# A hybrid trunk with RWKV-7 heads on one core: two pairs of heads per step, eight matrices per inverse

## The chip, the cores and the metric

One core of one Trainium2 chip runs the whole program. The metric is the device time of one execution in microseconds (us), lower is better. The engines are named as in the profile: PE (TensorE, matrix products), PEld (its weight loads), DVE (VectorE), ACT (ScalarE), POOL (GpSimd) and SP (SyncE, which issues the DMAs). PE writes into PSUM banks of 512 fp32 numbers per partition, and the other engines read them from there.

## The reference

A decoder trunk of two layers, width 2048, 256 tokens, all in float32. Each layer is a sequence mixer and a feed-forward part, each followed by a residual addition and a layer normalisation. Layer 0 mixes with multi-head latent attention (8 heads) and RWKV-7 (16 heads of 64), layer 1 with a gated DeltaNet and retention. The change is about the RWKV-7 heads, which the reference computes one token at a time:

```python
def step(st, inp):
    r_t, w_t, k_t, v_t, a_t, b_t = inp
    sa = jnp.einsum('bhvk,bhk->bhv', st, a_t)
    st = st * w_t[:, :, None, :] + sa[..., None] * b_t[:, :, None, :] + v_t[..., None] * k_t[:, :, None, :]
    return st, jnp.einsum('bhvk,bhk->bhv', st, r_t)
```

`r`, `k` and `v` are projections of the input, mixed with the token before (a shift); the decay `w`, the rate inside `b` and a gate `g` come from three low-rank projections. The result of each head is normalised over its 64 numbers (group norm), gets a bonus term from r, k and v, is multiplied with the gate and goes through the output projection together with the attention heads.

## The kernel before

Weights. All weights stream from HBM in blocks of eight 128x128 tiles into three buffers (`wr`), issued by SP. ACT rounds each half block to `wh` (L264), DVE or POOL computes the rest `wl` (L268), and PE makes three matmuls with 256 columns for each tile (L358 to L360): the stream. A group of 16 tiles of depth ends in one of two PSUM banks with the tag `mm`.

RWKV heads. `pair_mix` treats a pair of heads (128 partitions) at a time, over the 256 tokens in two chunks of 128. Its stages, each ended by a `yield`:

- `lw`, `la`, `lg` (L1094 to L1101): low-rank products for decay, rate and gate; ACT takes tanh; DVE sums the decay along time (two scans); ACT's exponentials give `e1`, `e2`. From these come `rAR`, `rb0`, `rkt` and `rt3`.
- Score products `rbig` (L1147): for each head, which takes one half of the 128 rows (partitions 0 to 63 or 64 to 127), a tile of one bank with both chunks. ACT copies and scales, POOL masks them into `rNB` and `rKA`.
- `tri_inv`: the inverse of the four 128x128 unit triangular matrices (2 heads x 2 chunks). ACT and POOL gather the 32x32 diagonal blocks, four small DMAs (L735) lay them out on 16 partitions, DVE eliminates in 14 steps of two instructions (L753, L754), four DMAs (L760) bring them back, and six `step`s of small matmuls (`tps`, L774) with DVE work between them assemble the inverse `tri_xt`: four with 32x32 blocks, two with 64x64.
- `rG`, `ru`, `rS`, `ry` (L1180 to L1207): chunk by chunk the products with the inverse, the state `rST` between the chunks, the output `ry`.
- Group norm on DVE (L1254 to L1261), transposes `ryt` (L1213), the bonus `rbon` (L1217), the gate and the split into `o0h` and `o0l`, which are inputs of the output projection.

The banks of PSUM: `c0` and `c1` with two each, one tag for even and one for odd pairs, `sm` two, `mm` two. `run_rolling` keeps two pairs alive at once, started 11 steps apart; each runs at a high priority, and one step of the attention heads (`side`) is taken in between. The program is put in order by a tile scheduler that takes the instructions of the highest priority that are ready by its model, so that stream matmuls stand between the stages of the pairs. Most buffers of `pair_mix` are double, r, k and v triple (`shift`, tag `sh_r` and so on).

Output projection. `out_part` multiplies some of the 16 input tiles with the weights and adds the result to `xf` on DVE (L854). The parts: tiles 0 to 3 and 4 to 7 (attention) within the attention heads, 8 to 11 behind the fourth pair, 12 and 13 behind the last, and last 14 and 15, in which the sums of the layer normalisation are taken along for each of the 16 columns (on POOL `accE`, L422; the column's split for the next phase, `rawl`, L537).

Mixer 1 uses `tri_inv` too, with four matrices at a time.

Of the kernel before, what the change touches and what calls it, by code (L numbers as in the profile page):

```python
# [16 lines left out]
P = 128  # L17
# [256 lines left out]
class K:  # L274
# [55 lines left out]
    def bank(self, tag, name):  # L330
        return self.psum.tile([P, 512], F32, name=name, tag=tag, bufs=self.banks[tag])
# [15 lines left out]
    LAG0 = 11  # L347
    LAG1 = 9
    BANKS0 = dict(c1=2, c0=2, sm=2, mm=2)
# [356 lines left out]
    def tri_persist(self, pool, n):  # L706
        v = self.nc.vector
        self.tri_slots = []
        for i in range(n):
            xt = pool.tile([P, 4, P], F32, name=f"tri_xt{i}")  # L710
            v.memset(xt, 0.0)
            x64 = pool.tile([64, 4, 64], F32, name=f"tri_x64{i}")
            v.memset(x64, 0.0)
            self.tri_slots.append((xt, x64))
        self.tri_n = 0

    def tri_inv(self, pool, nt, name, bank):


# [7 lines left out]
        c32 = pool.tile([P, 4, 32], F32, name=f"tc_{name}", tag="tc", bufs=1)  # L727
# [5 lines left out]
        q = pool.tile([16, self.QW], F32, name=f"tq_{name}", tag="tq", bufs=1)  # L733
        for h in range(4):
# [10 lines left out]
        for s in range(1, 15):  # L745
            n = 15 - s
            tmp = pool.tile([16, 2, 8, 8], F32, name=f"te_{name}_{s}", tag="te", bufs=2)
            t4 = tmp.rearrange("p k a b -> p k (a b)")[:, :, :s * n].rearrange("p k (c t) -> p k c t", c=s)
            z = qk[:, :, 0:512].rearrange("p k (c t) -> p k c t", t=32)
            col = z[:, :, 0:s, s:s + 1].broadcast_to([16, 2, s, n])  # L750
            row = qk[:, :, 32 * s + s + 1:32 * s + 16].unsqueeze(2).broadcast_to([16, 2, s, n])
# [6 lines left out]
        zc = pool.tile([P, 4, 32], F32, name=f"tz_{name}", tag="tc", bufs=1)  # L758
        for h in range(4):
            nc.sync.dma_start(zc[:, h, :], q[4 * h:4 * h + 4, :1024].rearrange("b (s t) -> b s t", t=32))  # L760
        x = pool.tile([P, 4, 32], F32, name=f"tx_{name}", tag="tx", bufs=2)
# [7 lines left out]
        def step(nm, n, ops):  # L769
            ps = bank(f"tps_{name}_{nm}")  # L770
            o = ps[:, :4 * n].rearrange("p (h c) -> p h c", h=4)
            for po, lhs, rhs in ops:
                for h in range(4):
# [4 lines left out]
        vv = pool.tile([P, 4, 32], F32, name=f"tv_{name}_16", tag="tv", bufs=2)  # L778
        v.tensor_tensor(vv, o, self.c("lev16x").unsqueeze(1).broadcast_to([P, 4, 32]), ALU.mult)
# [7 lines left out]
        vv = pool.tile([P, 4, 32], F32, name=f"tv_{name}_32", tag="tv", bufs=2)  # L787
# [4 lines left out]
        w = pool.tile([P, 4, 32], F32, name=f"tw_{name}", tag="tw", bufs=1)  # L792
# [9 lines left out]
        v6 = pool.tile([P, 4, 64], F32, name=f"tv64_{name}", tag="tv64", bufs=1)  # L802
        v.tensor_copy(v6[hi], o[hi])
        o = step("w64", 64, [(hi, xt[hi, :, hi], v6[hi])])
        w6 = pool.tile([P, 4, 64], F32, name=f"tw64_{name}", tag="tw64", bufs=1)
# [36 lines left out]
    def out_part(self, l, kts, last=False):  # L842


        kts = kts[::-1]
# [3 lines left out]
        for g in out_groups():  # L849
            outs = [self.bank("mm", f"pso{l}_{kts[0]}_{c}")[:, :T] for c in g]  # L850
            self.proj(st, f"l{l}_w_out", g, kts, oh, ol, outs)
            for c, o in zip(g, outs):
                with self.tc.high_priority(self.HP if last else 0):
                    self.nc.vector.scalar_tensor_tensor(  # L854
                        self.xf[c], self.xf[c], 1.0 if self.residual else ALPHA, o, ALU.mult, ALU.add)
                    if last:
                        self.ln_tile(f"m{l}", c)
        self.residual = True

    def out_tile(self, l, kt, slot):  # L860

        hl = [self.op.tile([P, T], F32R, name=f"o{l}{n}{kt}", tag=f"o{n}{slot}", bufs=1) for n in "hl"]
# [4 lines left out]
    def mixer0(self):  # L867
        tc = self.tc
        with ExitStack() as ctx:
            self.phase(ctx, "m0", **self.BANKS0)  # L870
# [4 lines left out]
            self.out_part(0, [14, 15], last=True)  # L875
            self.ln_finish("m0", "l0_ln1_g", "l0_ln1_b")

    def shift(self, pool, ps, i, name, tag=None):
# [5 lines left out]
        o = pool.tile([P, T], F32, name=f"sh_{name}", tag=tag or f"sh_{name}", bufs=3 if tag else 1)  # L884
# [3 lines left out]
    def mixer0_heads(self, st):  # L888
# [3 lines left out]
        with ExitStack() as ctx:  # L892
# [23 lines left out]
            self.tri_persist(kp, 2)  # L916
            sts = [kp.tile([P, P], F32, name=f"rST{i}") for i in range(2)]
            for t in sts:
                nc.gpsimd.memset(t, 0.0)
# [4 lines left out]
            def pair_proj(j, ps=None):  # L924
                r = []
                for n, kind in enumerate("rkv"):
# [776 lines left out]
```

## Time and profile before

| | us |
|---|---|
| median of 3 runs | 2534.15 (2530.69 to 2551.15) |
| profiled execution | 2534.57 |
| its span in the trace | 2532.2 |
| PE busy in the span | 2445.3 |
| DVE busy in the span | 1713.9 |

The program's phases follow each other in the trace: the first mixer from 0 to about 530 us, its feed-forward part to about 1320, the second mixer to about 1757, then the second feed-forward part. In a timeline row the first number is the start, the second how long the instructions took together, then engine, line, operation, output<-inputs, the tile of PE (rows*columns), the shape and the number of records; in brackets what an engine waited for. A matmul in full fp32 (the small ones) has two records, a stream matmul one. PE's matmuls are pipelined: their durations overlap, and the price of one is read from start to start.

### The profile page before, as it was taken

How to read it: one execution, taken by the hardware profiler on the slowest of the kernel's cores; microseconds unless marked ns; L12 is line 12 of the kernel's file. 1: busy time of each engine (PE TensorE's matmuls, PEld its weight loads, DVE VectorE, ACT ScalarE, POOL GpSimd, SP SyncE). 2: the span in 40 equal slices, each digit the busy share in tenths (PEclk: the TensorE clock that was granted, in tenths of full speed). 3: DMA queues.
4: the chain of work that ended last, by engine and by line, in shares of the span. 5: the costliest groups of instructions: out<-in, count | busy, mean ns of one | idle time of the engine just before them, and what ended most of it. 6: DMA issues, size and time to landing. Idle time of an engine off the chain costs nothing.

```text
span 2532.2 us, 52523 instructions
## 1 busy us (share of the span) xinstructions
PE 2445.3 (97%) x20516; PEld 2357.9 (93%) x20516; DVE 1713.9 (68%) x3579; ACT 1338.7 (53%) x2643; POOL 483.5 (19%) x592
## 2 busy tenths in 40 slices
PE   8999999889999999999979999999999999999996
PEld 7888889789999999999979888999899999999996
DVE  6777667778666666555578787758866666665555
ACT  6455454357555555544445454446655555554443
POOL 3333343253000000000044233236300000000001
PEclk9999999989999999999989999999999999999998
DMA  6333323325555556555534444544455555555553
GB/s 211 126 98 100 107 97 117 119 93 182 191 186 190 188 188 190 188 189 189 187 127 145 144 136 144 184 167 142 161 199 191 186 189 191 186 190 188 188 191 126
DMA packets 129417, 412.13 MB, mean 163 GB/s; under 512 B 25488, under 2 KB 30224, under 8 KB 129168
## 3 DMA queue, kind: packets, MB, share of 16 engines
q1 hardware_dynamic: 129168, 408.77, 48.8%
q8 instruction: 161, 2.64, 0.4%
q14 instruction: 88, 0.72, 0.1%
HBM read 405.04 MB, written 2.10 MB: 161 GB/s over the span
## 4 chain that ended last, share of the span: by engine, by line
PE 82%; DVE 9%; DMA 2%; ACT 2%; issue 2%; POOL 2%; SPq 1%; POOLq 0%; ACTq 0%; DVEq 0%
PE psd L358 6%; PE psd L359 6%; PE psd L360 6%; PE ps_l_ffn_w_val L359 6%; PE ps_l_ffn_w_val L360 6%; PE ps_l_ffn_w_gate L360 6%; PE ps_l_ffn_w_val L358 6%; PE ps_l_ffn_w_gate L359 6%; PE ps_l_ffn_w_gate L358 6%; PE pso L358 2%; PE pso L359 2%; PE pso L360 2%; DVE wl_m L268 2%; PE rbig L1147 1%; DVE wl_f L268 1%
## 5 line engine op out<-in xcount | busy, mean ns | idle before, releaser
L268 DVE TENSOR_TENSOR wl_f<-wr_f,wh_f 128x512 fp32r<-128x512 f32 (+1 forms) x1040 | 736.6, 710 | 530.3 <-ACT wh_f L264 530.2
L264 ACT ACTIVATE wh_f<-wr_f 128x512 fp32r<-128x512 f32 (+1 forms) x1056 | 652.9, 621 | 633.4 <-PE psd L360 233.5
L264 ACT ACTIVATE wh_m<-wr_m 128x512 fp32r<-128x512 f32 x464 | 289.8, 629 | 253.9 <-PE pso L360 78.8
L359 PE MATMUL psd<-hh,wl_f 128*128 128x256 f32 x1408 | 393.0, 279 | 0.0
L358 PE MATMUL psd<-hh,wh_f 128*128 128x256 f32 x1408 | 392.8, 279 | 0.0
L360 PE MATMUL psd<-hl,wh_f 128*128 128x256 f32 x1408 | 392.8, 279 | 0.0
L358 PE MATMUL ps_l_ffn_w_gate<-xh,wh_f 128*128 128x256 f32 x1216 | 339.6, 279 | 0.0
L359 PE MATMUL ps_l_ffn_w_gate<-xh,wl_f 128*128 128x256 f32 x1216 | 339.4, 279 | 0.0
L358 PE MATMUL ps_l_ffn_w_val<-xh,wh_f 128*128 128x256 f32 x1216 | 339.2, 279 | 0.0
L360 PE MATMUL ps_l_ffn_w_gate<-xl,wh_f 128*128 128x256 f32 x1216 | 339.2, 279 | 0.0
L359 PE MATMUL ps_l_ffn_w_val<-xh,wl_f 128*128 128x256 f32 x1216 | 339.2, 279 | 0.0
L360 PE MATMUL ps_l_ffn_w_val<-xl,wh_f 128*128 128x256 f32 x1216 | 339.2, 279 | 0.0
L268 POOL TENSOR_TENSOR wl_m<-wr_m,wh_m 128x512 fp32r<-128x512 f32 x154 | 214.5, 1393 | 377.5 <-ACT wh_m L264 309.3
L268 DVE TENSOR_TENSOR wl_m<-wr_m,wh_m 128x512 fp32r<-128x512 f32 x310 | 223.8, 724 | 75.3 <-ACT wh_m L264 68.5
L359 PEld LDWEIGHTS psd<-hh,wl_f 128*128 128x128 f32 x1408 | 264.7, 188 | 0.0
L360 PEld LDWEIGHTS psd<-hl,wh_f 128*128 128x128 f32 x1408 | 264.7, 188 | 0.0
L358 PEld LDWEIGHTS psd<-hh,wh_f 128*128 128x128 f32 x1408 | 264.6, 188 | 0.0
L359 PEld LDWEIGHTS ps_l_ffn_w_gate<-xh,wl_f 128*128 128x128 f32 x1216 | 228.5, 188 | 0.2
L358 PEld LDWEIGHTS ps_l_ffn_w_gate<-xh,wh_f 128*128 128x128 f32 x1216 | 228.6, 188 | 0.1
L359 PEld LDWEIGHTS ps_l_ffn_w_val<-xh,wl_f 128*128 128x128 f32 x1216 | 228.6, 188 | 0.0
L360 PEld LDWEIGHTS ps_l_ffn_w_gate<-xl,wh_f 128*128 128x128 f32 x1216 | 228.6, 188 | 0.0
L358 PEld LDWEIGHTS ps_l_ffn_w_val<-xh,wh_f 128*128 128x128 f32 x1216 | 228.6, 188 | 0.0
(641 smaller groups left out, 5493.8 us busy)
## 6 DMA issues: line engine op xcount, KB each, us to landing
wr_f<-w_f SPq DMA_DIRECT2D x526, 512.0 KB
wr_m<-w_m SPq DMA_DIRECT2D x230, 512.0 KB
xf<-x SPq DMA_DIRECT2D x7, 256.0 KB
rwl<-lora SPq DMA_DIRECT2D x8, 192.0 KB
rdt<-rdecay SPq DMA_DIRECT2D x4, 384.0 KB
y<-xf SPq DMA_DIRECT2D x5, 256.0 KB
wr_m<-w_m SPq DMA_DIRECT2D x4, 256.0 KB
wr_f<-w_f SPq DMA_DIRECT2D x4, 256.0 KB
```

Of the source, the lines that this page charges most:

```text
L264: nc.scalar.activation(self.hi[:, a], raw, AF.Copy)
L268: i = eng.tensor_tensor(self.lo[:, a], raw, self.hi[:, a].bitcast(F32), ALU.subtract)
L358: mm(out, hi, xh, start=first, stop=False)
L359: mm(out, lo, xh, start=False, stop=False)
L360: mm(out, hi, xl, start=False, stop=last)
L1147: mm(pb[:, T * cc:T * cc + T], src[rr, cc * P:cc * P + P], AR[rr, cc].rearrange("p a t -> p (a t)"), start=True, stop=True)
```

## The change

- `mix2` takes the place of `pair_mix`: four steps, each with two pairs (four heads, eight triangular matrices). The elimination's 14 steps run once for eight matrices on 32 partitions; there are eight small DMAs each way.
- One such step is alive at a time (`beside` lists what runs beside each of the four). There is one slot of the inverse's tiles, and r, k, v and the work tiles have one buffer (`bufs=1`). Some tiles share one: `thw` and `tha` with those of the inverse and of the group norm, `rSe` with `tq`, `rt3` with `ry`.
- PSUM: the tags `c0` and `c1` become `cc`, two tiles of two banks each.
- The score products of a pair and a kind go into one tile of two banks, one bank for each head, and the loops alternate between the heads, that is the row halves.
- In `tri_inv`'s `step` the loop over the matrices is outside and that over the blocks inside; one more `yield` stands before the last step. This holds for mixer 1 too.
- The bonus `rbon` moves ahead of the inverse. The group norm runs over eight groups, 512 columns.
- The output parts are: tiles 0 to 3 beside the third step, 8 to 11 and 4 to 7 beside the fourth, and last 12 to 15.

The core of the diff:

```diff
--- before
+++ after
 def bank(self, tag, name):
-        return self.psum.tile([P, 512], F32, name=name, tag=tag, bufs=self.banks[tag])
+        return self.psum.tile([P, 1024 if tag == "cc" else 512], F32, name=name, tag=tag, bufs=self.banks[tag])
...
 def tri_inv
-        for h in range(4):
+        for h in range(nm):
             nc.sync.dma_start(q[4 * h:4 * h + 4, :1024].rearrange("b (s t) -> b s t", t=32), c32[:, h, :])
...
-            tmp = pool.tile([16, 2, 8, 8], F32, name=f"te_{name}_{s}", tag="te", bufs=2)
+            tmp = pool.tile([P, 2, 8, 8], F32, name=f"te_{name}_{s}", tag="te", bufs=2)[:np_]
...
-            for po, lhs, rhs in ops:
-                for h in range(4):
+            for h in range(nm):
+                for po, lhs, rhs in ops:
                     mm(o[po, h, :], lhs[:, h, :], rhs[:, h, :], start=True, stop=True)
...
+        yield
         o = step("w64", 64, [(hi, xt[hi, :, hi], v6[hi])])
...
 def mixer0
-            self.phase(ctx, "m0", **self.BANKS0)
+            self.phase(ctx, "m0", cc=2, sm=2, mm=2)
...
-            self.out_part(0, [14, 15], last=True)
+            self.out_part(0, [12, 13, 14, 15], last=True)
...
+            def proj2(d, ps=None):
+                r = pj[d] = [kp.tile([P, 2, T], F32, name=f"sh_{k}{d}", tag=f"sh_{k}", bufs=1) for k in "rkv"]
+                for p in range(2):
+                    for n, kind in enumerate("rkv"):
...
+                        self.shift(kp, o, 8 * n + j, f"{kind}{j}", r[n][:, p, :])
+                        yield
...
-                def tl(nm, shape=None, bufs=2):
-                    return rp.tile(shape or [P, T], F32, name=f"{nm}{j}", tag=nm, bufs=bufs)
+                def tl(nm, n=2 * T, tag=None, bufs=1):
+                    return rp.tile([P, n], F32, name=f"{nm}{d}", tag=tag or nm, bufs=bufs)
...
-                    for h in range(2):
-                        rr = slice(64 * h, 64 * h + 64)
-                        pb = bank(f"rbig{j}{h}{int(sc)}")
-                        for cc in range(2):
-                            mm(pb[:, T * cc:T * cc + T], src[rr, cc * P:cc * P + P],
-                               AR[rr, cc].rearrange("p a t -> p (a t)"), start=True, stop=True)
+                    for p in range(2):
+                        pb = bank(f"rbig{d}{p}{int(sc)}")
+                        for cc in range(2):
+                            for h in range(2):
+                                mm(pb[:, 512 * h + T * cc:512 * h + T * cc + T], src[hh(h), p, chunk(cc)],
+                                   AR[hh(h), p, cc].rearrange("p a t -> p (a t)"), start=True, stop=True)
...
+                self.group_norm(rp, py[:, :512].rearrange("p (g n) -> p g n", g=8), y.rearrange("p (g n) -> p g n", g=8),
+                                64, 64e-5, f"r{d}", 8, ("tv64", "tw64"))
...
-            self.run_rolling(lambda j: pair_mix(j, pj[j]), 8, self.LAG0, before, side, after)
-            self.out_part(0, [12, 13])
+            beside = [[mla_setup(dd), proj2(1)],
+                      [heads(0), proj2(2)],
+                      [heads(1), proj2(3), part([0, 1, 2, 3])],
+                      [heads(2), heads(3), part([8, 9, 10, 11]), part([4, 5, 6, 7])]]
+            for d in range(4):
+                mix = mix2(d, pj[d])
+                def step():
+                    with tc.high_priority(self.HP):
+                        return next(mix, self) is not self
+                more = step() and step()
+                for side in beside[d]:
+                    for _ in side:
+                        more = more and step()
+                while more:
+                    more = step()
```

Score products, the first ones on PE (the names: `rbig`, pair or step, head or pair, kind; `psr1`, `pscq0`: stream). Before, a head's tile with two matmuls:

```order
L1147 MATMUL rbig001_1125<-rAR0_1111,rb00_1114 128x256 x2
L1147 MATMUL rbig011_1131<-rAR0_1111,rb00_1114 128x256 x2
L360 MATMUL psr1_634<-xl0_85,wh_m0_12_0_637 128x256
...
L358 MATMUL psr1_634<-xh7_76,wh_m0_12_1_653 128x256
L1147 MATMUL rbig000_1137<-rAR0_1111,rkt0_1115 128x256 x2
L359 MATMUL psr1_634<-xh7_76,wl_m0_12_1_654 128x256
L360 MATMUL psr1_634<-xl7_92,wh_m0_12_1_653 128x256
L358 MATMUL psr1_634<-xh8_77,wh_m0_13_0_671 128x256
L359 MATMUL psr1_634<-xh8_77,wl_m0_13_0_672 128x256
L1147 MATMUL rbig010_1142<-rAR0_1111,rkt0_1115 128x256 x2
L360 MATMUL psr1_634<-xl8_93,wh_m0_13_0_671 128x256
```

Now, a pair's tile with four:

```order
L358 MATMUL pscq0_967<-xh3_72,wl_m0_18_0_971 128x256
L1188 MATMUL rbig001_908<-rAR0_889,rb00_894 128x256 x4
L1188 MATMUL rbig011_918<-rAR0_889,rb00_894 128x256 x4
L359 MATMUL pscq0_967<-xl3_88,wh_m0_18_0_970 128x256
...
L359 MATMUL pscq0_967<-xl9_94,wh_m0_19_0_1004 128x256
L1188 MATMUL rbig000_928<-rAR0_889,rkt0_895 128x256 x4
L357 MATMUL pscq0_967<-xh10_79,wh_m0_19_0_1004 128x256
...
L358 MATMUL pscq0_967<-xh12_81,wl_m0_19_1_1021 128x256
L1188 MATMUL rbig010_936<-rAR0_889,rkt0_895 128x256 x4
L359 MATMUL pscq0_967<-xl12_97,wh_m0_19_1_1020 128x256
```

The four matmuls of a row alternate between the two heads of a pair (`rbig001` and `rbig011` are the two pairs of step 0); before, the two matmuls of a row belonged to one head, and two heads stood in adjacent rows in some places only.

The first product of the inverse on PE. Before, for the first pair:

```order
L1161 MATMUL rtk1_2220<-cb_64,sh_v1_854 128x128 x2
L774 MATMUL tps_r0_v16_1688<-tx_r0_1682,rNB0_1123 32x32 x16
L1161 MATMUL rtk1_2220<-cb_64,rkt1_2165 128x128
...
L359 MATMUL psk2_930<-xh6_75,wl_m0_20_1_950 128x256
L774 MATMUL tps_r0_w16_1707<-tv_r0_16_1705,tri_xt0_449 32x32 x16
L360 MATMUL psk2_930<-xl6_91,wh_m0_20_1_949 128x256
```

Now, for the first two pairs:

```order
L357 MATMUL psr2_1473<-xh3_72,wh_m0_28_0_1476 128x256
L780 MATMUL tps_r0_v16_1655<-tx_r0_1649,rNB0_906 32x32 x32
L358 MATMUL psr2_1473<-xh3_72,wl_m0_28_0_1477 128x256
...
L359 MATMUL psr2_1473<-xl9_94,wh_m0_29_0_1510 128x256
L780 MATMUL tps_r0_w16_1763<-tv16_r0_1688,tri_xt0_449 32x32 x32
L357 MATMUL psr2_1473<-xh10_79,wh_m0_29_0_1510 128x256
```

A row that had 16 matmuls has 32.

The end of one piece of heads and the start of the next on PE, where r and k of a later one are in the stream (`psk`, `psv`). Before, between the third pair's end (`ryt2`) and the fifth pair's start (`lw4`):

```order
L358 MATMUL psv4_2741<-xh1_70,wh_m0_48_0_2744 128x256
L1213 MATMUL ryt2_3924<-cb_64,ry2_3896 128x128 x2
L1217 MATMUL rbon2_3928<-rt32_2858,cb_64 128x256
L359 MATMUL psv4_2741<-xh1_70,wl_m0_48_0_2745 128x256
L360 MATMUL psv4_2741<-xl1_86,wh_m0_48_0_2744 128x256
...
L360 MATMUL psv4_2741<-xl5_90,wh_m0_48_1_2760 128x256
L774 MATMUL tps_r3_w32_4109<-tv_r3_32_4106,tri_xt1_453 32x32 x8
L1094 MATMUL lw4_4395<-sh_lora0_464,rwl4_4393 128x256
L358 MATMUL psv4_2741<-xh6_75,wh_m0_48_1_2760 128x256
```

Now, between the second step's end (`ryt1`) and the third step's start (`lwa2`, `rbig201`):

```order
L358 MATMUL psk6_3757<-xh15_84,wl_m0_59_1_3811 128x256
L359 MATMUL psk6_3757<-xl15_100,wh_m0_59_1_3810 128x256
...
L1262 MATMUL ry1_3171<-rST_453,rAR1_2236 128x128
L1269 MATMUL ryt1_3218<-cb_64,ry1_3190 128x128
L1123 MATMUL lwa2_3237<-sh_lora0_458,rwl2_3235 128x256
L1124 MATMUL lwa2_3237<-sh_lora0_458,rwl2_3235 128x256
...
L1269 MATMUL ryt1_3218<-cb_64,ry1_3190 128x128 x3
...
L1160 MATMUL rst2_3265<-cb_64,rsq1_2_3270 128x2 x2
L1188 MATMUL rbig201_3296<-rAR2_3277,rb02_3282 128x256 x4
L357 MATMUL psv6_3855<-xh0_69,wh_m0_60_0_3858 128x256
```

Before, stream matmuls (`psv4`) stand on both sides of `ryt2` and up to `lw4`. Now there is none between `psk6` and `psv6`; the rows left out belong to `rG`, `rS`, `ru`, `ry`, one attention head (`pst3`, `psoh3`), `lg2` and `rst2`.

## Rows read from the trace of the kernel before

**Rows 1.** The page's span and busy times by engine.

```profile
span 2532.2 us, 52523 instructions
...
PE 2445.3 (97%) x20516; PEld 2357.9 (93%) x20516; DVE 1713.9 (68%) x3579; ACT 1338.7 (53%) x2643; POOL 483.5 (19%) x592
...
PE 82%; DVE 9%; DMA 2%; ACT 2%; issue 2%; POOL 2%; SPq 1%; POOLq 0%; ACTq 0%; DVEq 0%
```

**Rows 2.** Windows: stretch, length, busy of five engines, granted clock, DMA share, GB/s.

```profile
0.00:530.00 530.00, 493.54 (x4161) 440.00 (x4162) 378.59 (x1027) 274.72 (x622) 191.51 (x287) 0.97 0.36 118
...
500.00:550.00 50.00, 38.30 (x231) 34.58 (x231) 36.51 (x82) 25.27 (x68) 29.51 (x32) 0.80 0.25 85
1130.00:1180.00 50.00, 50.00 (x431) 50.00 (x430) 29.23 (x44) 23.73 (x40) 2.94 (x4) 1.00 0.56 188
```

**Rows 3.** PE by line and shape, 0 to 530 us: busy, mean ns, idle before.

```profile
L1147 PE MATMUL rbig<-rAR,rkt 64*128 64x256 f32 x64 | 16.1, 404 | 0.0
L1147 PE MATMUL rbig<-rAR,rb 64*128 64x256 f32 x64 | 14.9, 402 | 0.4 <-DVE rga L1123 0.4
...
L774 PE MATMUL tps_r_v<-tx_r,rNB 32*32 32x32 f32 x384 | 12.0, 194 | 4.3 <-DVE tx_r L762 4.3
```

**Rows 4.** Timeline of PE at five places: low-rank and score products in the stream.

```profile
147.21 0.70 PE L1094 MATMUL lw<-sh_lora,rwl 64*128 64x256 f32 x2
...
155.80 1.13 PE L1147 MATMUL rbig<-rAR,rb 64*128 64x256 f32 x4
...
199.54 1.14 PE L1147 MATMUL rbig<-rAR,rb 64*128 64x256 f32 x8
200.61 0.39 PE L358 MATMUL psq<-cqh,wh_m 128*128 128x256 f32 x1
...
441.83 0.28 PE L359 MATMUL psv<-xh,wl_m 128*128 128x256 f32 x1
442.04 1.13 PE L1147 MATMUL rbig<-rAR,rb 64*128 64x256 f32 x4
443.10 0.43 PE L1206 MATMUL ry<-ru,rNB 128*128 128x64 f32 x2
```

**Rows 5.** Timeline of PE: two runs of the inverse's products in the stream.

```profile
288.27 0.89 PE L774 MATMUL tps_r_v<-tx_r,rNB 32*32 32x32 f32 x32
289.09 0.38 PE L358 MATMUL pso<-o0h,wh_m 128*128 128x256 f32 x1
289.31 0.28 PE L359 MATMUL pso<-o0h,wl_m 128*128 128x256 f32 x1
...
486.81 0.59 PE L774 MATMUL tps_r_w<-tv_r,tri_xt 32*32 32x32 f32 x16
487.44 0.35 PE L358 MATMUL pso<-o0h,wh_m 128*128 128x256 f32 x1
```

**Rows 6.** What PE waited for, 20 to 530 and 530 to 560 us: total, times, longest.

```profile
PE ryt L1213 <- DVE ry L1261: 6.4, 2, 5.2
PE tps_r_v L774 <- DVE tx_r L762: 4.3, 3, 2.0
...
PE pso L358 <- ACT o0h L327: 2.9, 3, 2.3
PE pso L358 <- DVE xf L854: 2.7, 5, 1.0
...
PE lnst_m L440 <- POOL accE_m L422: 2.5, 1, 2.5
```

**Rows 7.** Timelines of DVE and PE at the end of the last pair.

```profile
503.48 0.42 DVE L1254 TENSOR_REDUCE gm_r<-ry 128x4 f32<-128x256 f32 x1 [1.66 <-PE ry L1207]
...
508.66 0.66 PE L1213 MATMUL ryt<-cb,ry 128*128 128x128 f32 x2 [5.22 <-DVE ry L1261]
...
512.47 0.58 PE L358 MATMUL pso<-o0h,wh_m 128*128 128x256 f32 x1 [2.29 <-ACT o0h L327]
```

**Rows 8.** DVE by line, 0 to 530 us: elimination and the output parts' additions.

```profile
L753 DVE TENSOR_TENSOR te_r<-tq_r 16x28 f32<-16x28 f32 (+6 forms) x112 | 40.3, 360 | 7.2 <-DMA tq_r<-tc_r 5.7
L754 DVE TENSOR_TENSOR tq_r<-tq_r,te_r 16x28 f32<-16x28 f32 (+6 forms) x112 | 36.1, 322 | 1.8
...
L854 DVE SCALAR_TENSOR_TENSOR xf<-xf,pso 128x256 f32<-128x256 f32 x80 | 32.5, 411 | 7.7 <-PE pso L360 7.2
```

**Rows 9.** Timeline of SP: the inverse's DMAs on the way to the elimination.

```profile
259.81 2.43 SPq L735 DMA_DIRECT2D tq_r<-tc_r  x4
```

**Rows 10.** Timeline of POOL in the last output part.

```profile
536.02 1.05 POOL L537 TENSOR_TENSOR rawl_m<-rawf_m,rawh_m 128x256 fp32r<-128x256 f32 x1
537.03 0.92 POOL L422 TENSOR_TENSOR accE_m<-accE_m,xf 128x256 f32<-128x256 f32 x1
537.91 0.91 POOL L537 TENSOR_TENSOR rawl_m<-rawf_m,rawh_m 128x256 fp32r<-128x256 f32 x1
```

More of the change, by code (lines that the diff above doesn't have):

```diff
@@ L842, in out_part, with out_part_steps @@
     def out_part(self, l, kts, last=False):
+        for _ in self.out_part_steps(l, kts, last):
+            pass
+    def out_part_steps(self, l, kts, last=False):
         kts = kts[::-1]
@@ new lines, in mix2 @@
+                nc.scalar.activation(cw.unsqueeze(2), two(S)[:, :, P - 1:P], AF.Exp, scale=-KAPPA)
+                pst = bank(f"rst{d}")
+                for p, j in enumerate(js):
+                    sq = tl(f"rsq{p}_", T, "tx", 2)
+                    nc.scalar.activation(sq, Kx[:, p, :], AF.Square, scale=self.p("k_k", j))
+                    for cc in range(2):
+                        n = 4 * p + 2 * cc
+                        mm(pst[:, n:n + 2], sq[:, chunk(cc)], self.c("headsel"), start=True, stop=True)
@@ L1167, in pair_mix @@
+                pB = bank(f"rbon{d}")
+                for p in range(2):
+                    mm(pB[:, T * p:T * p + T], self.c("blk64"), t3[:, p], start=True, stop=True)
+                bv = tl("rbv")
+                v.tensor_tensor(two(bv), two(pB[:, :512]), V, ALU.mult)
                 yield
                 xt = None
-                for xt in self.tri_inv(rp, NB[:, :, 0, :], f"r{j}", bank):
+                for xt in self.tri_inv(rp, NB[:, :, 0, :], f"r{d}", bank, 8):
                     yield
-                def hh(h):
-                    return slice(64 * h, 64 * h + 64)
@@ new lines, in mix2 @@
+                    G = tl("rG", T)
+                    v.tensor_copy(G, pG[:, :T])
+                    pu = bank(f"ru{d}{cc}")
+                    for p in range(2):
+                        for h in range(2):
+                            s = slice(P * p + 64 * h, P * p + 64 * h + 64)
+                            mm(pu[:, s], xt[:, 4 * p + 2 * cc + h, :], G[:, s], start=True, stop=True)
+                    u = tl(f"ru{cc}", T)
+                    v.tensor_copy(u, pu[:, :T])
+                    us.append(two(u))
@@ L1245, in mixer0_heads, with heads, part @@
-            self.out_part(0, [12, 13])
-    def group_norm(self, pool, src, dst, n, eps, name):
+            dd = {}
+            def heads(i):
+                for _ in mla_pair(i, dd):
+                    yield
+            def part(kts):
+                yield from self.out_part_steps(0, kts)
+            pj = {}
+            for _ in proj2(0, ps[3]):
+                pass
+            beside = [[mla_setup(dd), proj2(1)],
+                      [heads(0), proj2(2)],
+                      [heads(1), proj2(3), part([0, 1, 2, 3])],
+                      [heads(2), heads(3), part([8, 9, 10, 11]), part([4, 5, 6, 7])]]
@@ L1254, in group_norm @@
+        sq, yc = (pool.tile([P, ng * n], F32, name=f"{t}_{name}", tag=t, bufs=1).rearrange("p (g n) -> p g n", g=ng)
+                  for t in tags)
         v.tensor_reduce(mean, src, AX.X, ALU.add)
         v.tensor_scalar(mean, mean, -1.0 / n, None, ALU.mult)
[L1256 removed]
+        v.tensor_tensor(yc, src, mean.unsqueeze(2).broadcast_to([P, ng, n]), ALU.add)
         nc.scalar.activation(sq, yc, AF.Square)
```

337 lines of the change are left out of this document (169 added, 168 removed).

## The prediction

> **What bounds the kernel now.** I read the busy times first, then the windows, then the waits and timelines of the stretches that the change touches.
>
> The busy times [rows 1] show TensorE (PE) occupied for 2445.3 of 2532.2 us, with 82% of the chain of waits; VectorE (DVE) is next with 68%. So a microsecond counts if PE does less, or waits less. The windows [rows 2] give PE's own price: between 1130 and 1180 us it ran nothing but stream matmuls (the 128x256 products of streamed weights), 431 in 50.00 us, or 0.116 us each at full granted clock. The first mixer, 0 to 530 us, is where nearly all of the change lies: there PE was busy 493.5 of 530 us. Its last part is worse: from 500 to 550 us 38.3 of 50 busy, at a granted clock of 0.80.
>
> The rows of PE by line [rows 3] give the small work of the RWKV heads: the score products (`rbig`) take 31.0 us for 64 matmuls, each recorded twice. The timelines [rows 4, 5] show how such a group stands in the stream. The waits [rows 6] say what PE lacked: mostly DVE, once each for a normalised `ry` (5.2 us) and for an output half (2.3 us), both at the end of the mixer [rows 7].
>
> The profiled execution took 2534.57 us for a span of 2532.2, and the median of the three runs is 2534.15; I add my sum to the median, the two being 0.4 us apart.
>
> **Score products: -10.5.** The order of before has 26 visits of `rbig`: in 6 of them the two heads of a pair stand together, in 20 one head stands alone. Rows 4 show both kinds. Eight records (two row halves) run from 199.54 to 200.61, 1.07 us; four records of one half run from 442.04 to 443.10, 1.06 us. So the two halves of the rows really run side by side when their outputs lie in different banks; a head alone pays the same for half the work. Before: 6 x 1.07 + 20 x 1.06 = 27.6. After: every tile holds both heads in two banks, alternating, 16 tiles x 1.07 = 17.1. The gain is 10.5. Bounds: from the busy sums, 31.0 - 16 x 1.14 = 12.8 gained; if alternating made the halves run one after the other, 16 x 2.12 = 33.9, a loss of 6.3. I take 10.5, as row 199.54 is the same pair of operands and shapes.
>
> **Inverse of mixer 0: -9.** The same number of matmuls comes in 24 runs per mixer in place of 48. Rows 5: 32 records last 0.89 us, 16 last 0.59, so a record costs 0.019 and a run 0.29 besides. 24 x 0.29 = 7.0. From the starts of what follows (0.82 and 0.63) the fixed part would be 0.44, or 10.6. Alternating the blocks, so that neighbours lie in different 32-row strips, may overlap more; I add 2 for it. Bounds: 5 (24 x 0.194, the mean duration of one such matmul [rows 3], as if only its drain were saved) to 12.5 (10.6 and the 2).
>
> Rows 5 show two more strips and 16 more records adding only 0.30 us, with all outputs of a step in one bank. The Trainium skill (TensorEngine Tiling (Array Packing), Restrictions and Gotchas) says that different row tiles cannot use one PSUM bank at a time. By that rule alternating strips gives nothing here, since one step's eight matrices all lie in one bank, while the score products, which get a bank per half, keep their gain. The sum by it would be 2 us later; the trace can't tell, as before never alternates within a bank.
>
> **Fewer switches: -4.** Stream to small matmul: 441.83 to 442.04 is 0.21 us against 0.116, so 0.09 on entering [rows 4]. The order counts 252 changes of tile shape in mixer 0 before and 168 after: 42 visits less, 42 x 0.09 = 3.8. Bounds 0 to -8 (leaving costs as much, 289.09 to 289.31).
>
> **Inverse of mixer 1: -1.** It keeps four matrices and gets only the alternation and one more yield (0 to -4.5).
>
> **DVE: -3.** The elimination's 224 instructions (40.3 + 36.1 us [rows 8]) become 112 on twice the partitions, so 38 us less DVE. Four output parts in place of five save 16 additions of 0.411 us. This is off the path except where PE waits for DVE: `tx` 4.3, `xf` 2.7 [rows 6]. I take under half, bounds 0 to -8.
>
> **DMAs, priced at nothing.** Per inverse there are eight small DMAs each way in place of four: the four issue in 2.43 us on SP [rows 9], so eight in about 4.9, and a weight load queued behind starts 2.4 us later. The three weight buffers hide that: each holds eight blocks of three matmuls, 24 x 0.116 = 2.8 us of stream. Without them it would be 4 x 2 x 2.4 = 19 us, which is in the rival below.
>
> **Boundaries: +23.** This is the price. Before, two pairs were alive with buffers of their own, and the order always had stream beside one pair's end and the next one's start. Now one chain of two pairs is alive and r, k, v, `rAR`, `rNB`, `rKA` are single. The order shows the consequence between steps 1 and 2: after the last matmul of `psk6` PE finishes step 1 and starts step 2 with no stream matmul between, because both `mm` banks hold `psr6` and `psk6`, whose results may only go into r and k after step 2 has read the old ones. What lies there: the normalisation chain, which from its first reduction at 503.48 to the transpose at 508.66 took 5.2 us for 256 columns [rows 7], for 512 by estimate 6; then `lwa` to score products, where the shortest seen is 147.21 to 155.80, 8.6 us [rows 4]; less some 2 us of PE work in it: about 13 idle. At the next boundary some 50 stream matmuls stand between, 50 x 0.116 = 5.8 us, so a stall of about 4. At the end the same wait as today (5.2 + 2.3 [rows 7]) grows by the wider normalisation: 3. Between steps 0 and 1 there is enough stream: nothing. Such a wait was followed by a low clock at 513 us (0.80 over rows 2's stretch), so I add 3 for stretches at 1.2 GHz. Sum 13 + 4 + 3 + 3 = 23. Bounds: +8 (PE work fills most of it) to +65 (rival B).
>
> **Tail: -2.** The last output part covers four heads, so each column takes 12 matmuls (1.4 us) in place of 6. Beside it POOL adds and splits each column in about 1.9 us (541.79 to 542.79 and the one before [rows 10]) and the sums behind wait for it 2.5 us [rows 6]. More PE work beside that chain hides the wait: -2, bounds 0 to -5.
>
> Sum: -10.5 - 9 - 4 - 1 - 3 + 23 - 2 = -6.5, which is 2534.15 - 6.5, near 2528 us.
>
> **Rivals.** A, boundaries covered: PE's order is fixed, but if the chain is shorter than I think (normalisation and score preparation partly side by side), the boundaries cost 8, and the alternation brings its upper bounds: -12.8 - 12.5 - 4 - 2 - 5 + 8 - 2 = -30, 2504 us. For it: the small mean waits today. Against: the row of 8.6 us was the shortest for half the width.
>
> B, the single chain rules (the other side): at every boundary DVE must do normalisation, scans and preparation for two pairs in a row while PE has both banks full. With 24 us at the 1-2 boundary, 18 at 2-3, 10 at 0-1, 8 at the end (65 with 5 for the clock), the gains of 29.5 turn into +35, 2569 us. It decides once the stalls together exceed 30. For it: the eight DMAs lengthen each inverse by 2 x 2.4 us. Against: 50 matmuls of cover at 2-3.
>
> C, alternation brings nothing: the score halves run one after the other and the strips too, so the first term is +6.3 and the second -7: +6.3 - 7 - 4 - 3 + 23 - 2 = +13, 2547 us. Row 199.54 speaks against it.
>
> **How the numbers follow.** A measurement of this kernel tells about 1%, 25 us, from no change. Forecast 0.52 (2528, its own range 2512 to 2545), A 0.26 (2504), B 0.14 (2569), C 0.08 (2547). Faster by over 1% (below 2509): most of A and a little of the forecast, 0.28. Slower (above 2559): B and a little of C, 0.15. Within: 0.57. The range leaves out the outer parts of A and B: 2492 to 2560.
>
> **What would show it.** Score products: 16 groups of eight records near 1.1 us. Inverse: 24 runs; x64 records below 1.6 us means alternation helps, near 1.8 that it doesn't. Boundaries: a PE gap of about 13 us for `ryt1` and the first `rbig` of step 2, shorter at step 3, and a lower granted clock behind it. DVE's elimination at half its time. The forecast is wrong if those gaps together are under 10 us or over 35, or if PE's busy time in mixer 0 doesn't fall by about 20.

## The result and the profile after

| | before | after |
|---|---|---|
| median | 2534.78 us (4 runs, 2530.69 to 2551.15) | 2507.59 us (4 runs, 2505.41 to 2512.94) |
| ratio | | 0.9884, 95% interval 0.9838 to 0.9930 |
| profiled span | 2532.2 us | 2503.7 us |

The changed kernel is 1.2% faster, 27 us; forecast were 6.5 us, with a range of 2492 to 2560 us. In a second measurement on another occasion (run after_again below) the ratio was 0.9865, 0.9837 to 0.9894, with a span of 2498.1 us.

The page after, the lines that answer to [rows 1]:

```profile
span 2503.7 us, 52076 instructions
...
PE 2406.7 (96%) x20516; PEld 2328.5 (93%) x20516; DVE 1662.3 (66%) x3265; ACT 1330.3 (53%) x2597; POOL 474.2 (19%) x515
```

PE has the same 20516 records and is busy 38.6 us less, while the span is only 28.5 us shorter. The gain is in PE's own work, not in fewer waits. The windows say where; as in [rows 2] the columns are stretch, length, busy of five engines, granted clock, DMA share, GB/s. First the mixer 0 of before, cut at the first matmul of the feed-forward part (529.3 us), then that of after, which ends at 502:

```profile
0.00:529.30 529.30, 492.84 (x4156) 439.31 (x4156) 377.89 (x1026) 274.02 (x620) 190.89 (x286) 0.97 0.36 119
```

```profile
0.00:502.00 502.00, 459.60 (x4157) 417.29 (x4158) 329.32 (x718) 269.34 (x587) 189.99 (x219) 0.96 0.39 125
...
250.00:300.00 50.00, 41.69 (x264) 33.93 (x264) 24.74 (x59) 23.62 (x56) 16.50 (x22) 0.83 0.16 47
450.00:500.00 50.00, 34.83 (x259) 33.11 (x258) 33.13 (x65) 27.17 (x69) 26.35 (x26) 0.87 0.26 85
```

Mixer 0 is 27.3 us shorter: PE's busy time fell by 33.2, its idle time rose from 36.5 to 42.4. The 50-us windows show where much of the idle time lies: around 264 us, the boundary between steps 1 and 2, and at the end, each with a granted clock of 0.83 to 0.87. The rest of the program adds only 1.2 us of gain (28.5 in all).

The small products of mixer 0 after, PE by line and shape, which answer to [rows 3]:

```profile
L1188 PE MATMUL rbig<-rAR,rb 64*128 64x256 f32 x64 | 9.7, 441 | 0.0
L1188 PE MATMUL rbig<-rAR,rkt 64*128 64x256 f32 x64 | 9.1, 402 | 0.0
...
L780 PE MATMUL tps_r_w<-tv_r,tri_xt 32*32 32x32 f32 x384 | 6.3, 193 | 0.0
L780 PE MATMUL tps_r_v<-tx_r,rNB 32*32 32x32 f32 x384 | 5.8, 193 | 1.9 <-DVE tx_r L767 1.8
L780 PE MATMUL tps_r_w<-tv_r,tri_xt 64*64 64x64 f32 x64 | 5.4, 224 | 0.0
L780 PE MATMUL tps_r_v<-tri_x,rNB 64*64 64x64 f32 x64 | 4.6, 221 | 0.0
```

Score products: 31.0 us before, 18.8 now. Inverse: 12.0 + 12.0 + 6.9 + 5.4 = 36.3 before, of which the tables of [rows 3] show the first; now 22.1. A run of 64 records in the timeline of PE, which answers to [rows 5]:

```profile
113.65 0.28 PE L359 MATMUL psr<-xl,wh_m 128*128 128x256 f32 x1
113.86 0.75 PE L780 MATMUL tps_r_w<-tv_r,tri_xt 32*32 32x32 f32 x64
114.54 0.39 PE L357 MATMUL psr<-xh,wh_m 128*128 128x256 f32 x1
```

From the start of this run to the start of the next matmul 64 records take 0.68 us; before, 32 took 0.82. Twice the work takes less time than the single work did.

The waits of PE after, 20 to 530 us (what waited, for what, total, times, longest), beside [rows 6]:

```profile
PE ryt L1269 <- DVE ry L1332: 13.1, 2, 6.5
PE pso L357 <- ACT xh L327: 3.9, 1, 3.9
PE psoh L1091 <- ACT pt L1088: 2.9, 2, 2.3
...
PE pso L358 <- POOL wl_m L268: 2.8, 2, 1.9
PE tps_r_v L780 <- DVE tx_r L767: 1.8, 3, 0.7
PE pso L357 <- DVE xf L865: 1.4, 3, 0.9
...
PE rG L1231 <- ACT rST L1251: 0.4, 2, 0.2
```

The wait for the normalised `ry` stands there twice with 6.5 us, once at the boundary 1 to 2 and once at the end, while the waits within the steps (`tx`, `xf`, `rST`) fell to about half or less. New are waits in the attention heads (`psoh` for `pt`) and, in the last output part, for weights that POOL splits (`wl_m`). The boundary in PE's timeline:

```profile
264.22 0.44 PE L1262 MATMUL ry<-rST,rAR 128*128 128x128 f32 x2
271.21 0.45 PE L1269 MATMUL ryt<-cb,ry 128*128 128x128 f32 x1 [6.54 <-DVE ry L1332]
271.58 0.79 PE L1123 MATMUL lwa<-sh_lora,rwl 64*128 64x256 f32 x1
...
275.33 1.22 PE L1136 MATMUL lg<-sh_lora,rwl 128*128 128x256 f32 x2 [0.84 <-ACT tha L1131]
...
281.73 2.08 PE L1188 MATMUL rbig<-rAR,rb 64*128 64x256 f32 x8
283.74 0.58 PE L357 MATMUL psv<-xh,wh_m 128*128 128x256 f32 x1
```

6.54 us of wait, then 12.5 us with small products only, until the stream goes on at 283.74; of these PE waits for another 0.84. The eight records of `rbig` take 2.0 us here, twice the usual 1.06: the clock had fallen behind the wait (0.58 granted from 265 to 285 us).

### The profile page after: what moved, and what is told of

Same layout as the page of the kernel before. It is cut to its first block, busy times and chain, and to the rows that moved or that the text cites. A ratio compares the mean times of both kernels' runs of the same rounds, so it can differ in the third digit from the quotient of the medians.

```text
span 2503.7 us, 52076 instructions
## 1 busy us (share of the span) xinstructions
PE 2406.7 (96%) x20516; PEld 2328.5 (93%) x20516; DVE 1662.3 (66%) x3265; ACT 1330.3 (53%) x2597; POOL 474.2 (19%) x515
## 4 chain that ended last, share of the span: by engine, by line
PE 70%; DVE 6%; POOL 1%; issue 1%; DMA 1%; ACT 1%; SPq 0%; DVEq 0%; ACTq 0%; POOLq 0%
PE psd L358 7%; PE psd L357 7%; PE psd L359 7%; PE ps_l_ffn_w_val L358 6%; PE ps_l_ffn_w_gate L358 6%; PE ps_l_ffn_w_gate L359 6%; PE ps_l_ffn_w_gate L357 6%; PE ps_l_ffn_w_val L359 6%; PE ps_l_ffn_w_val L357 6%; PE pso L357 1%; PE pso L358 1%; PE pso L359 1%; DVE wl_m L268 1%; DVE wl_f L268 1%; PE ps_l_ffn_w_val L355 1%
## 5 line engine op out<-in xcount | busy, mean ns | idle before, releaser
L268 DVE TENSOR_TENSOR wl_m<-wr_m,wh_m 128x512 fp32r<-128x512 f32 x310 | 232.9, 754 | 96.7 <-ACT wh_m L264 95.1
L359 PEld LDWEIGHTS ps_l_ffn_w_val<-xl,wh_f 128*128 128x128 f32 x1216 | 228.6, 188 | 0.0
```

Of the source, the lines that this page charges most:

```text
L268: i = eng.tensor_tensor(self.lo[:, a], raw, self.hi[:, a].bitcast(F32), ALU.subtract)
L359: mm(out, hi, xl, start=False, stop=last)
```

## The experiments

All times are medians; ratio and interval are against the kernel before on the same chip. The runs come from several chips, so ratios are to be compared, not microseconds.

| run | us | ratio | 95% interval |
|---|---|---|---|
| changed kernel | 2507.6 | 0.9884 | 0.9838 to 0.9930 |
| after_again | 2501.8 | 0.9865 | 0.9837 to 0.9894 |
| e1_blocks_outer | 2526.4 | 0.9967 | 0.9947 to 0.9987 |
| e2_halves_in_row | 2505.4 | 0.9882 | 0.9852 to 0.9912 |
| e4_before_alternating | 2527.5 | 0.9973 | 0.9957 to 0.9989 |
| e3_r_twice | 2514.6 | 0.9919 | 0.9885 to 0.9953 |
| e5_tail_split | 2502.0 | 0.9861 | 0.9835 to 0.9886 |
| e6_yield_m0_only | 2507.8 | 0.9885 | 0.9866 to 0.9904 |
| e7a_end_held | 2513.8 | 0.9909 | 0.9888 to 0.9929 |
| e7b_both_held | 2509.4 | 0.9891 | 0.9874 to 0.9909 |
| e9_no_groupnorm | 2488.5 | 0.9801 | 0.9779 to 0.9823 |
| e10_before_no_groupnorm | 2535.6 | 0.9990 | 0.9977 to 1.0004 |
| e8_split_and_yield | 2502.1 | 0.9860 | 0.9840 to 0.9880 |

**e1_blocks_outer.**

> The changed kernel with one thing undone: in the inverse's step the loop over the 32-row blocks is outside again and that over the matrices inside, in both mixers. Theory 1 (the inverse got cheaper than forecast because neighbouring matmuls in different row strips run together, all outputs of a step in one bank notwithstanding): in mixer 0 a run of 64 records takes about 1.4 us from start to start in place of 0.68, one of 32 records about 0.82 in place of 0.62, the runs of the 64x64 step stay at 1.07; PE's time for these products grows by 7 to 8 us in mixer 0 and by about 4 in mixer 1, where half of it or more is hidden; the whole kernel is 7 to 11 us slower than the changed kernel, about 2515 to 2518 us. Rival (it is the batch of eight matrices, with half as many runs, that pays): runs of 64 records stay below 0.9 us and the time stays within 2 us of 2507.6.

```diff
-            for h in range(nm):
-                for po, lhs, rhs in ops:
+            for po, lhs, rhs in ops:
+                for h in range(nm):
```

The timeline of PE, the same run as above:

```profile
112.67 0.27 PE L359 MATMUL psr<-xl,wh_m 128*128 128x256 f32 x1
112.88 1.91 PE L780 MATMUL tps_r_w<-tv_r,tri_xt 32*32 32x32 f32 x64
114.71 0.38 PE L357 MATMUL psr<-xh,wh_m 128*128 128x256 f32 x1
```

1.83 us in place of 0.68, and the whole kernel is slower by 0.8%, some 20 us. That is Theory 1, and more than it expected. 1.83 is also more than 2 x 0.82, so these runs save PE nothing by the batch of eight when they don't alternate. The products account for about 12 us of the 20: eight runs of 64 records by 1.15 and eight of 32 by 0.40. Mixer 0 ran at a granted clock of 0.93, against 0.96 in the changed kernel; why it was lower here was not tested:

```profile
0.00:520.60 520.60, 480.55 (x4156) 437.77 (x4157) 323.50 (x718) 270.11 (x587) 189.99 (x219) 0.93 0.37 120
```

**e2_halves_in_row.**

> The changed kernel with one thing undone: the four score products of a tile come as head 0 chunk 0, head 0 chunk 1, head 1 chunk 0, head 1 chunk 1, so that the row halves don't alternate; tiles, banks and the order of everything else are as in the changed kernel. Theory 2 (adjacency of the two halves with an output bank each is enough; in the trace of before eight records in this very order took 1.07 us): a tile's eight records stay at 1.06 us, and the time stays within 2 us of 2507.6. Rival (alternation is what lets them overlap): a tile takes 1.6 to 2.1 us, 16 tiles 8 to 17 us more, 2516 to 2525 us.

```diff
-                        for cc in range(2):
-                            for h in range(2):
+                        for h in range(2):
+                            for cc in range(2):
```

The timeline of PE, a tile of score products:

```profile
76.02 1.14 PE L1188 MATMUL rbig<-rAR,rkt 64*128 64x256 f32 x8
77.09 0.39 PE L359 MATMUL pscq<-xl,wh_m 128*128 128x256 f32 x1
```

1.07 us without alternation, and the time is that of the changed kernel: Theory 2. Since one head alone takes 1.06 us too [rows 4], what pays is that both heads' products come together; the order of the four doesn't matter. Each head has a bank of its own here; one bank for both was not run.

**e4_before_alternating.**

> The kernel before with the alternation alone: blocks inside and matrices outside in the inverse's step (both mixers), and the score products of a pair's two heads written chunk by chunk with the heads alternating, into two tiles of one bank as before; pairs, buffers, batches of four matrices and output parts are those of before. Theory 1: a run of 32 records takes about 0.38 us in place of 0.82, one of 16 about 0.37 in place of 0.52, so 8 x (2 x 0.44 + 2 x 0.15) = 9.4 us less PE time in mixer 0; the score products stay apart in most places of the order and gain 0 to 4; mixer 1 gives back most of its 4; in all 9 to 15 us faster than before, 2520 to 2526 us, that is one third to one half of the change's gain. Rival (batching and fewer buffers pay, alternation doesn't): within 3 us of before.

The step's loops as in the changed kernel, and in `pair_mix`:

```diff
+                    pbs = [bank(f"rbig{j}{h}{int(sc)}") for h in range(2)]
+                    for cc in range(2):
+                        for h in range(2):
+                            rr = slice(64 * h, 64 * h + 64)
+                            mm(pbs[h][:, T * cc:T * cc + T], src[rr, cc * P:cc * P + P],
...
```

The lines of PE by shape:

```profile
L1147 PE MATMUL rbig<-rAR,rb 64*128 64x256 f32 x64 | 15.5, 403 | 0.9 <-DVE rga L1123 0.9
L1147 PE MATMUL rbig<-rAR,rkt 64*128 64x256 f32 x64 | 14.1, 405 | 0.0
L774 PE MATMUL tps_r_w<-tv_r,tri_xt 32*32 32x32 f32 x384 | 8.8, 195 | 0.0
L774 PE MATMUL tps_r_v<-tx_r,rNB 32*32 32x32 f32 x384 | 7.8, 194 | 4.1 <-DVE tx_r L762 4.1
```

0.27% faster, about 7 us: Theory 1's direction, a little under its 9 to 15. The 32-wide products fell from 24.0 to 16.6. From start to start the whole inverse took 24.8 us, against 32.6 before and 20.0 in the changed kernel: alternation alone gives 7.8 of the 12.6, and eight matrices at a time the other 4.8, once the strips alternate. The score products stayed at 29.6 (31.0 before), since with single-bank tiles the order still set most heads apart.

**e3_r_twice.**

> The changed kernel with a second buffer for the shifted r of two pairs, so that one of the two PSUM banks of the stream comes free at the boundary between steps 1 and 2 and the 48 stream matmuls of the next v can run before the next step has read the old r. Theory 3 (the gap of 6.5 us before the transposes is the length of the chain of normalisation, and the stream that comes free is run earlier, beside the products before it, not in the gap): the gap stays at 6 to 7 us and the time within 3 us of 2507.6. Rival (the prediction's reason, that the held banks make the boundary): up to 48 x 0.116 = 5.6 us of the boundary is filled, and the stretch at the low clock behind it gets shorter by up to 4 us; 2498 to 2503 us.

```diff
-tag=f"sh_{k}", bufs=1) for k in "rkv"]
+tag=f"sh_{k}", bufs=2 if k == "r" else 1) for k in "rkv"]
```

```profile
271.76 0.45 PE L1269 MATMUL ryt<-cb,ry 128*128 128x128 f32 x1 [6.53 <-DVE ry L1332]
...
284.29 0.58 PE L357 MATMUL psr<-xh,wh_m 128*128 128x256 f32 x1
```

The wait before the transposes stayed at 6.53 us; the 48 stream matmuls of `psv` ran ahead of the products before it. So far Theory 3. The prediction's reason, the held banks, is neither shown nor refuted by it: the stream goes on behind the gap with the next `psr`, so by the order of the projections `psk` and `psv` hold both banks in it, and no stream was left to run there. The ratio is 0.9919, with a clock of 0.93 in mixer 0. Its interval overlaps that of the changed kernel, so a loss isn't shown.

**e5_tail_split.**

> The changed kernel with its last output part split again: tiles 12 and 13 first, then 14 and 15 with the sums of the normalisation. Theory 4 (twelve matmuls per column beside POOL's chain of about 1.9 us per column hide the wait that stood at the end of mixer 0, which is why the first feed-forward part is 5 us shorter than before): the wait of the sums (lnst) for POOL returns with 2 to 3 us, 16 more additions on DVE, 3 to 6 us slower than the changed kernel, 2511 to 2513 us. Rival (the shorter feed-forward part has another cause): within 2 us of 2507.6.

```diff
-            self.out_part(0, [12, 13, 14, 15], last=True)
+            self.out_part(0, [12, 13])
+            self.out_part(0, [14, 15], last=True)
```

The wait of `lnst` came back with only 0.5 us, the first feed-forward part stayed short (751.7 us), and the time isn't longer than the changed kernel's. Theory 4 falls. What the larger last part is worth by itself the time can't tell, because the split also changes other waits: that for the last `ry` fell to 1.8, and the 2.8 for `wl_m` at the end is gone.

**e6_yield_m0_only.**

> The changed kernel with the additional yield before the inverse's last product kept in mixer 0 alone, so that mixer 1 has its former stages and the alternation. Theory 5 (in mixer 1 the 4.4 us saved in the inverse's products come back as idle time because the additional stage lets the chain of the inverse end later: PE's wait of gu for tri_xt went from 1.7 to 3.5 us): mixer 1 gets 2 to 5 us shorter, 2503 to 2506 us. Rival (mixer 1 is bound by DVE's part of the chain, whatever the stages): mixer 1 stays at 471 to 472 us and the time within 2 us.

```diff
         v.tensor_copy(v6[hi], o[hi])
-        yield
+        if nm == 8:
+            yield
```

The wait of `gu` for `tri_xt` fell from 3.5 to 2.3 us and mixer 1 from 471.7 to 469.1, as Theory 5 says, but the kernel's time is the same (in the profiled execution the first feed-forward part was 8 us longer than the changed kernel's), and in e8 mixer 1 took 471.0 with this edit. Inconclusive.

**e7a_end_held and e7b_both_held.**

> The changed kernel with eight columns of the output part of tiles 4 to 7 queued on PE behind the last product of ry in step 3, so that stream matmuls stand where PE waits for the last normalisation. Theory 6 (the waits of 6.5 and 3.9 us at the end are places without stream, and the chain before them has slack because its products stand behind stream): both waits go or shrink to under 2 us, the low clock behind them (10 us at half) goes too, and nothing of it comes back earlier: 6 to 13 us faster than the changed kernel, 2495 to 2502 us. Rival (the chain sets the pace, and columns taken from before it leave gaps there): the waits move to earlier places and the time stays within 3 us of 2507.6.

> As the run before it, and the 48 stream matmuls of the seventh pair's k queued behind the last product of ry in step 1, so that they stand in the gap of the boundary between steps 1 and 2. Theory 6: the wait of 6.5 us before the transposes goes, and the 17 us at half clock behind it shrink: another 5 to 13 us, 2484 to 2496 us. Rival: the same matmuls are missing before ry, PE waits there for DVE in other places, and the time stays within 3 us of that of the run before it.

```diff
+                        with tc.issue_after(self.ry_last):
+                            for _ in side:
+                                pass
...
+                                with tc.issue_after(self.ry_last):
+                                    w_in((kind, j), o)
```

The waits of PE in e7a, then its timeline shortly before the place where the wait stood:

```profile
PE ryt L1269 <- DVE ry L1341: 6.5, 1, 6.5
PE pso L357 <- ACT xh L327: 3.2, 1, 3.2
...
PE rbig L1188 <- ACT rg L1139: 1.7, 1, 1.7
```

```profile
436.16 1.97 PE L1227 MATMUL rG<-rtk,rKA 128*128 128x64 f32 x8
439.29 1.97 PE L1239 MATMUL ru<-rG,tri_xt 128*128 128x64 f32 x8 [1.16 <-DVE rG L1234]
...
448.26 0.64 PE L1260 MATMUL ry<-rtk,rKA 128*128 128x64 f32 x2
448.68 0.63 PE L1261 MATMUL ry<-ru,rNB 128*128 128x64 f32 x2
```

One of the two waits of 6.5 us is gone, as Theory 6 wanted, and yet e7a isn't faster. The same products in the changed kernel:

```profile
457.79 0.39 PE L1260 MATMUL ry<-rtk,rKA 128*128 128x64 f32 x2
458.02 0.39 PE L1261 MATMUL ry<-ru,rNB 128*128 128x64 f32 x2
```

0.42 us from start to start in e7a, 0.23 there. The windows of this stretch, of the changed kernel and of e7a:

```profile
430.00:480.00 50.00, 38.03 (x340) 36.32 (x340) 29.59 (x68) 16.84 (x37) 11.23 (x10) 0.90 0.25 85
430.00:480.00 50.00, 43.93 (x307) 42.20 (x305) 24.80 (x58) 14.64 (x31) 8.28 (x8) 0.73 0.19 65
```

With the stream taken away the chain of small products stands alone, PE waits for DVE between them, and they run at half the clock: 0.73 granted in e7a against 0.90. In mixer 0 PE's idle time fell from 42.4 to 37.0 us and its busy time rose from 459.6 to 465.2. e7b (whose wait at the boundary shrank to 3.4) has the same clock of 0.73 there. What the wait gave, the clock took: the Rival, with another mechanism than it named.

**e9_no_groupnorm and e10_before_no_groupnorm.**

> The changed kernel without the group norm of the RWKV heads: ry is copied from PSUM instead, so that each of the four steps loses a chain of about 6 us on DVE. Theory 7 (the normalisation is what PE lacks at the ends of steps 1 and 3, and the low clock follows these stretches): the two waits of 6.5 us shrink to about 1, idle time in mixer 0 falls by 10 to 13 us, the stretches at half clock get shorter by 15 us or more, in all 15 to 25 us faster than the changed kernel, 2483 to 2493 us. Rival (the rest of the chain keeps the pace, as in the runs with held stream): the waits move on to the low-rank products and the score products, 3 to 10 us faster.

> The kernel before without the group norm of the RWKV heads: ry is copied instead, eight chains of about 5 us less on DVE. Theory 7: only the last one stood on PE's path (5.2 us of wait and the low clock behind it), so 6 to 14 us faster than before, 2523 to 2531 us; the difference to the gain of the changed kernel's run without it is what the single chain pays more at its boundaries. Rival (DVE's load is what slows the kernel before, 68% busy): 20 us or more.

```diff
-                self.group_norm(rp, py[:, :512].rearrange("p (g n) -> p g n", g=8), y.rearrange("p (g n) -> p g n", g=8),
-                                64, 64e-5, f"r{d}", 8, ("tv64", "tw64"))
+                v.tensor_copy(y, py[:, :512])
```

The changed kernel gains 0.64% without the norm (0.9801 against 0.9865 on the same chip), 16 us, or 13 by the medians; the kernel before gains 0.10% (interval -0.04 to 0.23), 2.5 us. Theory 7 had asked for 15 to 25 and for 6 to 14: it is met at its edge by the first and missed by the second. Mixer 0 of e9, then of e10:

```profile
0.00:484.20 484.20, 459.64 (x4156) 419.02 (x4156) 305.11 (x650) 267.53 (x583) 187.94 (x219) 0.96 0.40 129
0.00:522.20 522.20, 494.55 (x4157) 439.24 (x4157) 350.69 (x890) 271.56 (x611) 193.00 (x286) 0.97 0.38 120
```

Busy is unchanged (459.64 against 459.60 in the first profile), and all of the gain is idle time: 24.6 left of 42.4, with 1.0 us of wait for `ry` in place of 13.1. In e10 27.6 us of idle time are left of 36.5. So the normalisation costs the single chain more than the two chains of before: about 13 us by the ratios, 9 by the idle times, with several us of uncertainty. The clock, which Theory 7 expected to recover, stayed at 0.96.

**e8_split_and_yield.**

> A candidate: the changed kernel with the last output part split into tiles 12, 13 and then 14, 15, and the additional yield in mixer 0 alone. Theory: the parts of 12 and 13 stand beside the last normalisation (wait 1.8 in place of 6.5 us in the run of the split alone) and mixer 1 keeps its 2.6 us: 3 to 8 us faster than the changed kernel on the same chip. Rival (the low clock gives it back, as with the held columns): within 2 us of the changed kernel.

The two edits of e5 and e6 together: the same as the changed kernel on the same chip (0.9860 and 0.9865). Of the runs that leave nothing out, none is clearly faster than it.

**after_again.**

> The changed kernel itself beside the three others, for a second profile. Theory (the stretches at half clock in mixer 0 differ from one execution of the same order to the next): the records of mixer 0 are within 1 us of busy time outside such stretches, and the time at half clock differs from 37.5 us by 7 us or more; median 2503 to 2513 us. Rival (the order sets the clock): the stretches have the same places and lengths within 3.4 us.

The windows of the second profile:

```profile
0.00:497.30 497.30, 454.37 (x4156) 412.88 (x4157) 329.46 (x718) 267.83 (x584) 188.25 (x216) 0.97 0.39 126
...
430.00:480.00 50.00, 37.93 (x336) 36.37 (x330) 29.68 (x65) 19.04 (x43) 12.95 (x12) 0.86 0.22 75
```

The same order took 497.3 us at a mean clock of 0.97 after 502 at 0.96: one point of clock is 5 us. Of 430 to 480 us the clock was 0.86 here and 0.90 in the first profile; of 30 to 45 us it was 1.00 against 0.89, of 130 to 140 us 1.00 against 0.83. The longest waits are the same to a tenth (13.1 for `ry`, 3.9 for `xh`). In all 34 us of mixer 0 ran at the low clock here and 41 in the first profile, a difference of 7 us; from the 37.5 that the theory names it is half of that, so the theory's size is not met. That the order alone sets the clock doesn't hold either: some of the stretches are missing, while the idle time is the same.

## Why the prediction was right, and where it was not

The sign and the wide range held. The size was 6.5 us against 27, outside the forecast's own 2512 to 2545, and "faster by over 1%" had been given 0.28. The order of the terms did not hold: the boundaries, by far the largest term, cost about as much as the inverse or the switches gave. Of its signs, 64 records stayed below 1.6 us (0.68) and the elimination took half its time; the gap at the boundary 1 to 2 was 7.4 us in place of 13, and the two boundary gaps together 10.5, just above the 10 under which the forecast called itself wrong. By its own steps, with the records of mixer 0 of before and of the second profile after, which have the same mean clock of 0.97 (sums from start to start):

- Score products, -10.5: measured 28.1 to 18.1, -10.0. Right in size and reason; [rows 4] and e2 together show that the pair's adjacency does it.
- Inverse, -9 (7 from the fixed part of a run, 2 from alternation): measured 32.6 to 20.0, -12.6. The two parts were sized the wrong way round. I took 0.29 us per run as a cost that halving the runs would save. By e1 it is not: without alternation eight matrices cost 33.7 against before's 32.6, and even without the 1.8 that two runs at the low clock add, halving the runs saves only 0.7. Alternation alone is worth 7.8 (e4), and halving the runs adds 4.8 on top of it. The rule of the Trainium skill that I weighed here (TensorEngine Tiling (Array Packing), Restrictions and Gotchas: different row tiles cannot use one PSUM bank at a time) does not hold for these products: their four strips write one bank, each its own 32 partitions, and 64 records take 0.68 us alternating against 1.83 in a row.
- Fewer switches, -4: this is the step that was most mis-sized, but not all of the difference is switches. The stream's own matmuls, the same number, take 12.5 us less, the other small products 3.3 less, which no run explains. The visits did fall by 42 (135 to 93). I priced one at 0.09, its entry, and left the exit (0.10, [rows 5], 289.09 to 289.31) as a bound: 42 x 0.19 = 8.0. The other 4.5 us are in part the clock of the one execution: 60 stream matmuls ran at the low clock before, 25 in the second profile, but 67 in the first, whose stream is only 7.1 us shorter. At the full clock alone a stream matmul takes 0.131 us before and 0.127 to 0.128 after, 8 to 10 us over some 2500 of them. No run changes the number of visits by itself.
- Boundaries, +23: partly right. The wait of normalisation is there as said, 6.5 us twice. The waits add up to 13 us: 7.4 at the boundary 1 to 2 (6.54 + 0.84) for the 13 forecast there, 2.3 + 0.8 around the next for 4, and 2.9 more at the end (6.5 + 3.9 against 5.2 + 2.3) for 3; e9 against e10 gives 9 to 13. The step that failed is "less some 2 us of PE work": between `ryt` and the stream PE worked for all but 0.84 of 12.5 us. The 3 for the low clock came to nothing in the second profile (0.97 before and after), while the first was at 0.96. Whether the held banks are the reason that no stream stands there stays open (e3).
- DVE, -3: waits within the steps fell by about 7 us. PE's waits for DVE between 20 and 530 us, without those for `ry` and the first `sh_lora`, sum to 12.7 before and 5.7 after. It fits the total: all waiting of mixer 0 rose by 5.9 (36.5 to 42.4), of which 13 came at the boundaries. The elimination's time halved as said: 76.4 to 38.6 us.
- Tail, -2: the first feed-forward part, from its first matmul to its last, is 3 to 5 us shorter (757.0 before, 752.2 and 753.8 after), and PE no longer waits for `lnst`; but e5, which splits the tail again, keeps that, so the reason given is not shown. It stays open.
- Mixer 1, -1: products -4.4 us (16.68 to 12.24), given back as waits (24.5 to 30.1 us in the first profile); in all 470.8 to 471.7.

Together: -10.0 - 12.6 - 15.8 + 13 - 7 - 4 + 1 = -35, against 34.1 between the two spans. The forecast's error is 12 us in the switches (some 3 of them the clock), 10 in the boundaries, 4 in the inverse and 4 in DVE, all in one direction, so no luck among the terms hid it; that 2507.6 lay within the range is owed to the range's lower end, which took in most of rival A.

Rival A was the nearest in size, but not for its reason: the boundaries were not covered (13 against its 8). They were paid, and PE's work fell by more. Rivals B and C are refuted by the profile: the boundaries cost 13 us, and row halves and strips do run together.

## What to carry to other kernels

Small matmuls on 32-row strips should be written so that neighbours in the queue lie in different strips; here that was a change of two loops, and it was worth 0.8% with eight matrices at a time (a lower clock in that run included) and 0.3% with four. A visit of a dense stream by small work has a price on both sides (0.09 and 0.10 us in the rows), so fewer and longer visits should pay beyond the work itself; no run here tests that alone. A wait on the critical engine wasn't worth its length in e7a and e7b: filling it with work taken from elsewhere uncovered other small work, and the clock fell there instead.

## What was not expected of the hardware

- Four 32-row strips with outputs in the same bank: 64 records in 0.68 us, 11 ns each; in a row per strip 1.83 us, 29 ns each, and then eight in a row are slower than twice four (2 x 0.82).
- The clock of one and the same order differs between executions: mixer 0 at 0.96 and 0.97 in two profiles, each point about 5 us. The runs e1 and e3, other orders, were at 0.93. Chains of small products without stream between them ran at half pace (0.42 us from start to start against 0.23), with PE busy almost throughout: 43.93 of 50 us in e7a's window of 430 to 480 us, at a granted clock of 0.73.
